# Roots on GpSimd, squares and scalings on ScalarE, and a new deal of the input rows in a two-layer hybrid encoder

## The chip, the cores and the metric

The kernel runs on one core of a Trainium2 chip. The metric is the device time of one execution in microseconds. Before the change three runs took 916.98, 917.23 and 917.36 us; the median is 917.23.

Five engines work side by side in the core: TensorE (PE in the profile; its weight loads are PEld), VectorE (DVE), ScalarE (ACT), GpSimd (POOL) and SyncE (SP), which here only issues DMAs. Each has its own queue and works it off in order. An instruction that needs another engine's result waits at the head of its queue, and all behind it wait too.

## The reference

Two layers run over x (256 tokens of 2048 features, fp32). In each layer:

```python
h = rmsnorm(x, norm_g[l])
a_x, a_b, a_c, a_g, d_q, d_k, d_v, d_g, m_q, m_g = split(h @ w_in[l])   # 4 x 768, 4 x 768, 2 x 512 columns
# A: gated convolution over three tokens
y_a = a_b * conv3(a_c * a_x) * silu(a_g)
# D: six heads; q and k are normed in halves of 64 columns
s_c = q_c @ k_c.T / 8 - slope[h] * abs(i - j)                           # c = 0, 1
o = (softmax(s_0) - lam * softmax(s_1)) @ v
y_d = rmsnorm(o, head_g) * (1 - lam_init) * silu(d_g)
# M: four heads over 256 memory tokens; mq and mk are normed over 128 columns
y_m = softmax(mq @ mk.T / sqrt(128)) @ mv * silu(m_g)
x = x + concat(y_a, y_d, y_m) @ w_out[l]
```

The memory's keys and values are rmsnorm(mem) @ w_mem_kv[l]. Every rmsnorm is v * rsqrt(mean(v * v) + 1e-6) * gain.

## The kernel before

**Products in three parts.** All large products have 128x128 stationary tiles of the turned tokens (xT, yT, memT) and 512 moving columns of weights. Each fp32 operand is split in two: hi is the value rounded to fp32r (ScalarE, L294, or L899 and L892 in the memory's phase), and lo is the rest (VectorE, raw − hi, L295, L900 and L892). Three matmuls (hi hi, hi lo, lo hi) make one product.

**Blocks and chunks.** A block is 512 output columns of 256 tokens: two PSUM accumulators `acc`, one for each row tile t, and 16 k tiles of 128 features. Weights come in chunks of two k tiles (CK = 2), 512 KB each, by a DMA on SP (L291) into one of four `raw` buffers; hi and lo have four buffers each. So SP waits until a `raw` is free, ScalarE until a hi is free, VectorE for hi, TensorE for both. Four accumulators allow two blocks to be open. Where w_in has pieces of 256 columns, a chunk is two DMAs. In some places two k tiles of two blocks are done with seven products in place of eight (`seven`); there VectorE also forms sums of the weights (L380).

**Order in time.** The memory's products come first (about 0 to 98 us), then layer 0 (to about 500 us) and layer 1. In a layer the blocks go q and k (three blocks, b = 0, 1, 2, each normed in halves of 64), v and gates, then memory queries and gates, then the convolution's groups, then w_out. Beside the blocks run side tasks, Python generators that are called forward between chunks (`later`, `run_side`); they hold the heads, the turning of x, the memory's keys. What is marked `pin` or `keep_in_program_order` stays in the order of the code on its engine; the rest is placed by a scheduler when the program is built.

**What the change touches.**
- `rsqrt` (L189 to L204): a first guess by integer steps and three Newton steps on VectorE, 11 instructions; `Steps` lets some of them run between chunks.
- `row_stats` (L414 to L422): from the sum of squares of each token, r and five multiples of it.
- `normed_steps` (L436 to L447): for q, k and the memory's queries and keys: one square of 128x512 on ScalarE for each t, a grouped sum on VectorE, the roots, and one multiplication on VectorE from PSUM to an SBUF sheet. The accumulators come free behind it.
- `diff_weights` and `diff_out` (L613 to L646): for each head, the scores with the distance term, maximum, exponentials, and their combination; then the head's own norm, times the gate.
- `mem_scores` (L651 to L680): the same for the memory's heads.
- `x_turned`, `turn_strips` (L767 to L784): x in strips of 32 rows, turned by VectorE (L770), then each of four k tiles multiplied by its gain and split (L264, L265).
- `keys` (L845 to L857): the memory's keys go out and back over GpSimd's DMA queue (L852, L853) and are then turned by VectorE (L855) into mkT.
- `row_tiles`, `x_row_tiles`, `load_w`: which row of w_in goes to which partition, and the DMA of a chunk.

Of the kernel before, what the change touches and what calls it, by code (L numbers as in the profile page):

```python
# [48 lines left out]
def encoder(ctx: ExitStack, tc: tile.TileContext, x, mem, norm_g, w_in, conv_w, conv_b,  # L49
# [128 lines left out]
    class Steps:  # L178


        def __init__(self):
            self.ops = []

        def __getattr__(self, op):
            return lambda *a, **k: self.ops.append((op, a, k))

        def run(self, n):
            for at, (op, a, k) in enumerate(self.ops):
                tc.keep_in_program_order(getattr(nc.vector, op)(*a, **k))  # L189
                if at % n == n - 1:  # L190
                    yield 1

    def rsqrt(t, n, vec=None):

        vec = vec or nc.vector
        y = small.tile([P, n], F32, tag=f"rs_y{n}", name=nm("rsy"))
        a = small.tile([P, n], F32, tag=f"rs_a{n}", name=nm("rsa"))
        yi = y.bitcast(I32)
        vec.tensor_scalar(yi, t.bitcast(I32), 1, None, ALU.logical_shift_right)
        vec.tensor_scalar(yi, yi, -1.0, float(0x5F3759DF), ALU.mult, ALU.add)  # L200
        for _ in range(3):
            vec.scalar_tensor_tensor(a, y, -0.5, y, ALU.mult, ALU.mult)
            vec.tensor_tensor(a, a, t, ALU.mult)
            vec.scalar_tensor_tensor(y, a, 1.5, y, ALU.add, ALU.mult)  # L204
        return y

# [79 lines left out]
    def load_w(rows, cols):  # L286
# [3 lines left out]
        for lo, n in cols:  # L290
            nc.sync.dma_start(raw[:, :, at:at + n], rows[:, :, lo:lo + n])  # L291
            at += n
# [137 lines left out]
    def normed_steps(vec, acc, gs, st, home):  # L430

        ng = NB // gs
        ss = small.tile([P, NT, ng], F32, tag=f"ss{ng}", name=nm("ss"))
        for t in range(NT):
            sq = tmp.tile([P, NB], F32, tag="nat", name=nm("sq"), bufs=3)
            nc.scalar.activation(sq, acc[t], AF.Square)  # L436
# [931 lines left out]
```

## Time and profile before

| | |
|---|---|
| median of three runs | 917.23 us |
| the profiled execution: its span, first to last instruction | 916.3 us |
| granted clock of TensorE | 1.000 |
| TensorE busy | 910.9 us (99%) |
| VectorE busy | 733.0 us (80%) |
| ScalarE busy | 499.0 us (54%) |
| GpSimd busy | 38.2 us (4%) |
| DMA | 215.18 MB, mean 235 GB/s |

The time of the profiled execution is known by its span alone. In rows of the profile a name such as `hi<-raw` is output and input by the program's names; `[1.67 <-PE acc L305]` is the idle time of the engine just ahead of the instruction, and what ended it. In the table of windows an engine's busy time in a stretch stands with its number of instructions in brackets. A row of waits gives microseconds in total, times, and the longest.

### The profile page before, as it was taken

How to read it: one execution, taken by the hardware profiler on the slowest of the kernel's cores; microseconds unless marked ns; L12 is line 12 of the kernel's file. 1: busy time of each engine (PE TensorE's matmuls, PEld its weight loads, DVE VectorE, ACT ScalarE, POOL GpSimd, SP SyncE). 2: the span in 40 equal slices, each digit the busy share in tenths (PEclk: the TensorE clock that was granted, in tenths of full speed). 3: DMA queues.
4: the chain of work that ended last, by engine and by line, in shares of the span. 5: the costliest groups of instructions: out<-in, count | busy, mean ns of one | idle time of the engine just before them, and what ended most of it. 6: DMA issues, size and time to landing. Idle time of an engine off the chain costs nothing.

```text
span 916.3 us, 12514 instructions
## 1 busy us (share of the span) xinstructions
PE 910.9 (99%) x4203; PEld 753.2 (82%) x4203; DVE 733.0 (80%) x1321; ACT 499.0 (54%) x778; POOL 38.2 (4%) x68
## 2 busy tenths in 40 slices
PE   9999999999999999999999999999999999999998
PEld 6888888888888888888888888888888888888887
DVE  5579978878789778677689859888888789498786
ACT  5667644546546556545556544556545556456352
POOL 2435010000000000000000000000000000000000
PEclk9999999999999999999999999999999999999999
DMA  8899888786787998979777874996869998989842
GB/s 288 289 243 256 280 247 230 227 258 185 204 228 185 271 263 242 243 253 254 240 220 232 271 243 117 280 279 197 221 192 208 258 266 256 240 243 253 280 157 93
DMA packets 244050, 215.18 MB, mean 235 GB/s; under 512 B 131976, under 2 KB 171720, under 8 KB 243984
## 3 DMA queue, kind: packets, MB, share of 16 engines
q1 hardware_dynamic: 239008, 208.71, 78.9%
q0 software_dynamic: 3776, 4.59, 2.1%
q10 hardware_dynamic: 1200, 1.07, 0.3%
q8 instruction: 33, 0.54, 0.3%
q14 instruction: 33, 0.27, 0.1%
HBM read 193.30 MB, written 21.00 MB: 234 GB/s over the span
## 4 chain that ended last, share of the span: by engine, by line
PE 98%; DMA 1%; SPq 0%; DVE 0%; ACT 0%; issue 0%
PE acc L305 90%; PE x L351 2%; PE acc L351 2%; PE po L518 1%; PE s L608 1%; DMA raw<-in_w_mem_kv_dram 1%; PE po L733 1%; PE pt L747 0%; PE s L666 0%; PE s L667 0%; PE s L665 0%; SPq L880 0%; SPq L817 0%; DVE lo L900 0%; ACT hi L899 0%; PE rest L305 0%
## 5 line engine op out<-in xcount | busy, mean ns | idle before, releaser
L305 PE MATMUL acc<-hi,xT 128*128 128x512 f32 x1760 | 550.5, 390 | 0.0
L294 ACT CAST hi<-raw 128x1024 fp32r<-128x1024 f32 x266 | 278.5, 1052 | 281.3 <-PE acc L305 187.3
L295 DVE TENSOR_TENSOR lo<-raw,hi 128x1024 fp32r<-128x1024 f32 x266 | 323.6, 1220 | 113.3 <-ACT hi L294 111.7
L305 PEld LDWEIGHTS acc<-hi,xT 128*128 128x128 f32 x1760 | 330.2, 188 | 68.8
L305 PE MATMUL acc<-lo,xT 128*128 128x512 f32 x880 | 343.0, 390 | 0.0
L305 PEld LDWEIGHTS acc<-lo,xT 128*128 128x128 f32 x880 | 165.2, 188 | 33.1
L305 PE MATMUL acc<-hi,yT 128*128 128x512 f32 (+1 forms) x432 | 134.1, 388 | 0.0
L305 PEld LDWEIGHTS acc<-hi,yT 128*128 128x128 f32 x432 | 81.0, 188 | 16.7
L305 PE MATMUL acc<-lo,yT 128*128 128x512 f32 x216 | 83.7, 388 | 0.0
L305 PE MATMUL acc<-hi,memT 128*128 128x512 f32 x248 | 78.1, 393 | 0.0
L305 PEld LDWEIGHTS acc<-hi,memT 128*128 128x128 f32 x248 | 46.1, 188 | 9.4
L900 DVE SCALAR_TENSOR_TENSOR lo<-raw,cva,hi 128x1024 fp32r<-128x1024 f32 (+1 forms) x34 | 41.0, 1220 | 14.2 <-ACT hi L899 13.8
L305 PE MATMUL acc<-lo,memT 128*128 128x512 f32 x124 | 48.0, 391 | 0.2 <-DVE lo L900 0.2
L305 PEld LDWEIGHTS acc<-lo,yT 128*128 128x128 f32 x216 | 40.5, 188 | 8.4
L899 ACT ACTIVATE hi<-raw,cva 128x1024 fp32r<-128x1024 f32 (+1 forms) x34 | 36.5, 1099 | 11.3 <-DMA raw<-in_w_mem_kv_dram 9.7
L377 ACT CAST hi<-wide 128x1024 fp32r<-128x1024 f32 x21 | 21.8, 1050 | 27.1 <-DVE wide L380 12.3
L377 DVE TENSOR_TENSOR lo<-wide,hi 128x1024 fp32r<-128x1024 f32 x21 | 25.5, 1221 | 4.3 <-ACT hi L377 4.0
L305 PEld LDWEIGHTS acc<-lo,memT 128*128 128x128 f32 x124 | 23.3, 188 | 6.0 <-DVE lo L900 1.1
L622 ACT ACTIVATE e<-e,mx 128x256 f32<-128x256 f32 x48 | 23.8, 498 | 6.2 <-DVE mx L618 6.2
L764 POOL DMA_DIRECT2D xt<-in_x_dram x32 | 21.4, 677 | 19.5 <-DVE rsy L189 13.7
L480 DVE STREAM_TRANSPOSE sh<-sh 128x1024 f32<-128x1024 f32 (+2 forms) x14 | 17.4, 1239 | 0.0
L264 ACT ACTIVATE xT<-xf,gx 128x256 fp32r<-128x256 f32 x32 | 14.3, 500 | 4.8 <-DVE xf L770 4.1
(218 smaller groups left out, 760.0 us busy)
## 6 DMA issues: line engine op xcount, KB each, us to landing
raw<-in_w_in_dram SPq DMA_DIRECT2D x188, 512.0 KB, 4.8
raw<-in_w_out_dram SPq DMA_DIRECT2D x54, 512.0 KB, 4.8
raw<-in_w_in_dram SPq DMA_DIRECT2D x64, 256.0 KB, 4.3
raw<-in_w_mem_kv_dram SPq DMA_DIRECT2D x30, 512.0 KB, 6.0
d<-sh SPq DMA_DIRECT2D x88, 128.0 KB, 4.2
sh<-d SPq DMA_DIRECT2D x72, 128.0 KB, 4.2
wide<-in_w_out_dram SPq DMA_DIRECT2D x10, 512.0 KB, 6.3
xs<-in_x_dram SPq DMA_DIRECT2D x4, 512.0 KB, 6.2
```

The lines of the kernel that those rows point to most:

```text
L264: both = (nc.scalar.activation(hi, src, AF.Copy, scale=gain), nc.vector.scalar_tensor_tensor(lo, src, gain, hi.bitcast(F32), ALU.mult, ALU ...
L294: nc.scalar.copy(hi, raw)
L295: nc.vector.tensor_tensor(lo_, raw, hi.bitcast(F32), ALU.subtract)
L305: i = nc.tensor.matmul(acc, left, right, start=start, stop=stop)
L351: nc.tensor.matmul(acc, left[a], right[b], start=first and i == 0, stop=last and i == 2)
L377: return ((hi, pin(nc.scalar.copy(hi, src))), (lo, pin(nc.vector.tensor_tensor(lo, src, hi.bitcast(F32), ALU.subtract))))
L480: tc.keep_in_program_order(nc.vector.transpose(src, src))
L518: nc.tensor.matmul(po[:, t, :], eT[:, i, t, k, :], v[:, k, h * P:(h + 1) * P], start=k == 0, stop=k == NT - 1)
L622: nc.scalar.activation(e[:, c, i], e[:, c, i], AF.Exp, bias=mx[:, c, i:i + 1], accum_out=sm[:, c, i:i + 1])
L764: tc.keep_in_program_order(nc.gpsimd.dma_start(st[:, n], src[n * B:(n + 1) * B].rearrange("p (b r) -> b p r", b=NA)))
L899: both = (nc.scalar.activation(hi[:, j], raw[:, j], AF.Copy, scale=g), nc.vector.scalar_tensor_tensor(lo[:, j], raw[:, j], g, hi[:, j].bit ...
L900: nc.vector.scalar_tensor_tensor(lo[:, j], raw[:, j], g, hi[:, j].bitcast(F32), ALU.mult, ALU.subtract))
```

## The change

It does six things.

1. **Roots.** `rsqrt` becomes one GpSimd instruction, t to the power −0.5, with a tile of −0.5 as exponent. `row_stats` moves to GpSimd with it (six instructions).
2. **Norms of q, k, mq, mk.** In place of one square of 128x512 ScalarE makes one for each group (eight of 64 columns, or four of 128), each with its sum. GpSimd makes the mean and the root for each t. ScalarE then copies each group from PSUM to the sheet with the root as scale. VectorE has nothing left in it.
3. **Heads.** ScalarE makes the distance term of a head (128x512); VectorE adds it to the scores and takes the maximum in one instruction (four of 128x256). ScalarE scales the second softmax and VectorE adds the two at once. The head's norm goes over GpSimd (add, power, multiply), its scaling to ScalarE, and one VectorE multiplication with the gate is left. In the memory's heads the factor 1/sqrt(128) goes into a gain, and ScalarE scales the weights.
4. **Rows of w_in.** Within each group of 512 rows, partition 32 b + p of k tile j holds row 128 b + 32 j + p where it held row 4 (32 b + p) + j. The strips of x are then turned from contiguous columns, and norm_g is loaded by four DMAs and turned by VectorE.
5. **Strips of x.** Four gains in place on ScalarE, then one copy and one subtraction of 128x1024 for the whole strip, where each k tile had its own.
6. **Loads.** Each k tile of a chunk has its own DMA: 242 loads of 512 KB become two of 256 KB each, and 64 of 256 KB become two of 128 KB each.

In the built program TensorE has 4,155 matmuls before and after. ScalarE goes from 605 rows of the listing to 776, GpSimd from 36 to 155, and VectorE from 1,247 to 864 (a row can stand for several equal instructions).

**Where the order changes.** The first place is ScalarE at the first q block of layer 0. `hi` are the casts of weights, `sq` the squares, `acc` the block's accumulators, `sh` the sheet. Before:

```order
L294 CAST hi_1245<-raw_1243 128x1024
L294 CAST hi_1263<-raw_1261 128x1024
L294 CAST hi_1281<-raw_1279 128x1024
L436 ACTIVATE sq_1215<-acc_1061 128x512
L436 ACTIVATE sq_1219<-acc_1062 128x512
L294 CAST hi_1299<-raw_1297 128x1024
L294 CAST hi_1323<-raw_1321 128x1024
L294 CAST hi_1341<-raw_1339 128x1024
```

After the change:

```order
L276 CAST hi_1347<-raw_1344 128x1024
L418 ACTIVATE sq_1229,ss_1205<-acc_1050 128x64
L418 ACTIVATE sq_1231,ss_1205<-acc_1050 128x64
L418 ACTIVATE sq_1233,ss_1205<-acc_1050 128x64
L426 ACTIVATE sh_1243<-acc_1049,rs_1206 128x2x32 x3
L418 ACTIVATE sq_1235,ss_1205<-acc_1050 128x64
L426 ACTIVATE sh_1243<-acc_1049,rs_1206 128x2x32 x5
L276 CAST hi_1366<-raw_1363 128x1024
L418 ACTIVATE sq_1237,ss_1205<-acc_1050 128x64
L418 ACTIVATE sq_1239,ss_1205<-acc_1050 128x64
L276 CAST hi_1385<-raw_1382 128x1024
L426 ACTIVATE sh_1243<-acc_1050,rs_1206 128x2x32 x8
```

The scaled copies, which wait for GpSimd's root `rs`, now stand between the casts: those of the first tile behind squares of the second, those of the second tile behind a cast.

The second place is GpSimd's queue at the end of the memory's phase. `xt` are strips of x, `kd` and `sh` the way of the memory's keys out and back. Before:

```order
L764 DMA xt_716<-in_x_dram 128x1x128 x8
L764 DMA xt_801<-in_x_dram 128x1x128 x8
L852 DMA kd_928<-sh_617 32x4x256 x4
L853 DMA sh_617<-kd_928 128x1024
L852 DMA kd_1315<-sh_1028 32x4x256 x4
L853 DMA sh_1028<-kd_1315 128x1024
```

After the change:

```order
L419 TENSOR_SCALAR ss_1020<-ss_1020,stm_491 128x4
L188 TENSOR_TENSOR rs_1021<-ss_1020,root 128x4
L419 TENSOR_SCALAR ss_1205<-ss_1205,st_1040 128x8
L188 TENSOR_TENSOR rs_1206<-ss_1205,root 128x8
L419 TENSOR_SCALAR ss_1205<-ss_1205,st_1040 128x8
L188 TENSOR_TENSOR rs_1206<-ss_1205,root 128x8
L826 DMA kd_1300<-sh_1086 32x4x256 x4
L827 DMA sh_1086<-kd_1300 128x1024
L419 TENSOR_SCALAR ss_1421<-ss_1421,st_1040 128x8
L188 TENSOR_TENSOR rs_1422<-ss_1421,root 128x8
L419 TENSOR_SCALAR ss_1421<-ss_1421,st_1040 128x8
L188 TENSOR_TENSOR rs_1422<-ss_1421,root 128x8
```

The second layer's keys (`kd_1300`) now stand behind the roots of the first q block (`rs_1206`), where they stood directly behind the first layer's.

The third place is VectorE where the memory's phase ends. `lo` are the conversions for the first block of layer 0 (lo_979 and lo_1002 before, lo_976 and lo_1001 after are its chunks 0 and 1), `mkT` is the turn of the first layer's keys. Before:

```order
L422 TENSOR_TENSOR st_1038<-rsy_1041 128x2
L892 TENSOR_TENSOR lo_1002<-raw_976,hi_1001 128x1024
L770 STREAM_TRANSPOSE xf_1019<-xt_801 128x1024
L189 TENSOR_REDUCE ss_1021<-sq_1022 128x4
L892 TENSOR_TENSOR lo_1098<-raw_982,hi_1097 128x1024
L189 TENSOR_SCALAR ss_1021<-ss_1021,stm 128x4
L189 TENSOR_REDUCE ss_1021<-sq_1024 128x4
L892 TENSOR_TENSOR lo_1117<-raw_984,hi_1116 128x1024
L855 STREAM_TRANSPOSE mkT_111<-sh_617 128x1024
```

After the change:

```order
L875 SCALAR_TENSOR_TENSOR lo_957<-raw_929,cva,hi_956 128x1024
L762 TENSOR_TENSOR xT_112<-xf_911,xT_112 128x1024
L867 TENSOR_TENSOR lo_976<-raw_953,hi_975 128x1024
L829 STREAM_TRANSPOSE mkT_113<-sh_670 128x1024
L867 TENSOR_TENSOR lo_1001<-raw_972,hi_1000 128x1024
L748 STREAM_TRANSPOSE xf_1018<-xt_802 128x1024
L867 TENSOR_TENSOR lo_1092<-raw_979,hi_1091 128x1024
```

The turn of the keys moved from behind chunk 3 to between chunks 0 and 1.

The last place is SP in layer 1, where the 256-column blocks begin. `raw` are chunks of weights, the rest are sheets on their way through DRAM. After the change:

```order
L473 DMA d_6912<-sh_6501 32x4x256 x4
L477 DMA mqT_6243<-d_6912 128x8x32 x4
L273 DMA raw_7050<-in_w_in_dram 128x1x256 x4
L477 DMA yn_6554<-d_6995 128x4x32 x4
L273 DMA raw_7077<-in_w_in_dram 128x1x256 x4
L273 DMA raw_7104<-in_w_in_dram 128x1x256 x4
L273 DMA raw_7144<-in_w_in_dram 128x1x256 x4
L273 DMA raw_7165<-in_w_in_dram 128x1x256 x4
L473 DMA d_7186<-sh_7000 32x4x256 x4
L273 DMA raw_7191<-in_w_in_dram 128x1x256 x4
```

Each `raw` there is now four DMAs of 128 KB, where it was two of 256 KB.

The diff, cut to its core:

```diff
...
+BIG = 3.0e38
...
     def load_norm():
-        tc.keep_in_program_order(nc.gpsimd.dma_start(gx.rearrange("p (m j) -> p m j", j=QT),
-                                                     norm_g.rearrange("l (q p j) -> p (l q) j", p=P, j=QT)))
+        rows = norm_g.rearrange("l (q b j p) -> b (l q) j p", b=NA, j=QT, p=B)
+        for b in range(NA):
+            pin(nc.gpsimd.dma_start(gx[b * B:(b + 1) * B], rows[b]))
+        yield 4
+        pin(nc.vector.transpose(gx, gx))
...
-    def rsqrt(t, n, vec=None):
...
+    root = const.tile([P, NT * NB // HALF], F32, name="root")
+    nc.gpsimd.memset(root, -0.5)
+    def rsqrt(r, t):
+        n = t.shape[-1]
+        nc.gpsimd.tensor_tensor(r, t, root[:, 0:n], ALU.pow)
...
     def row_tiles(w, k):
-        return w[k * P:(k + CK) * P].rearrange("(j p) c -> p j c", p=P)
+        return [w[(k + j) * P:(k + j + 1) * P] for j in range(CK)]
     def x_row_tiles(w, k, n=CK):
         q, j = divmod(k, QT)
-        return w[q * NB:(q + 1) * NB].rearrange("(p j) c -> p j c", j=QT)[:, j:j + n]
+        tiles = w[q * NB:(q + 1) * NB].rearrange("(b j p) c -> b p j c", j=QT, p=B)
+        return [tiles[:, :, j + i] for i in range(n)]
...
         raw = raw_tile()
         at = 0
         for lo, n in cols:
-            nc.sync.dma_start(raw[:, :, at:at + n], rows[:, :, lo:lo + n])
+            for j, row in enumerate(rows):
+                nc.sync.dma_start(raw[:, j, at:at + n], row[..., lo:lo + n])
             at += n
...
+    R, HR, HR2, R2, ET = range(5)
     def row_stats(ss, tag):
-        st = keep.tile([P, 6, NT], F32, tag=tag, name=nm(tag))
+        st = keep.tile([P, 5, NT], F32, tag=tag, name=nm(tag))
         t = small.tile([P, NT], F32, tag="st_t", name=nm("stt"))
...
+        nc.gpsimd.tensor_scalar(t, ss, 1.0 / D_MODEL, EPS, ALU.mult, ALU.add)
+        rsqrt(st[:, R], t)
+        nc.gpsimd.tensor_scalar(st[:, ET], t, EPS, None, ALU.mult)
+        nc.gpsimd.tensor_scalar(st[:, HR], st[:, R], 0.5, None, ALU.mult)
+        nc.gpsimd.tensor_tensor(st[:, R2], st[:, R], st[:, R], ALU.mult)
+        nc.gpsimd.tensor_scalar(st[:, HR2], st[:, R2], 0.5, None, ALU.mult)
         return st
     def col(st, which, t):
         return st[:, which, t:t + 1]
-    def normed_steps(vec, acc, gs, st, home):
-        ng = NB // gs
+    def normed_steps(acc, gs, st, home):
+        ng, w = NB // gs, gs // B
         ss = small.tile([P, NT, ng], F32, tag=f"ss{ng}", name=nm("ss"))
+        r = small.tile([P, NT, ng], F32, tag=f"rs{ng}", name=nm("rs"))
         for t in range(NT):
-            sq = tmp.tile([P, NB], F32, tag="nat", name=nm("sq"), bufs=3)
-            nc.scalar.activation(sq, acc[t], AF.Square)
-            vec.tensor_reduce(ss[:, t], sq.rearrange("p (g d) -> p g d", d=gs), AX.X, ALU.add)
-            vec.tensor_scalar(ss[:, t], ss[:, t], col(st, R2_64 if gs == HALF else R2_128, t), EPS,
-                              ALU.mult, ALU.add)
-        r = rsqrt(ss.rearrange("p t g -> p (t g)"), NT * ng, vec).rearrange("p (t g) -> p t g", t=NT)
+            for g in range(ng):
+                sq = small.tile([P, gs], F32, tag="sq", name=nm("sq"), bufs=1)
+                nc.scalar.activation(sq, acc[t][:, g * gs:(g + 1) * gs], AF.Square, accum_out=ss[:, t, g:g + 1])
+            nc.gpsimd.tensor_scalar(ss[:, t], ss[:, t], 1.0 / gs, col(st, ET, t), ALU.mult, ALU.add)
+            rsqrt(r[:, t], ss[:, t])
+            yield 1
         both = home()
         for t in range(NT):
...
+            for g in range(ng):
+                j, b = divmod(g * w, NA)
+                nc.scalar.activation(both[:, b:b + w, j, t], strips(acc[t][:, g * gs:(g + 1) * gs]), AF.Copy,
+                                     scale=r[:, t, g:g + 1])
+            yield 1
         return both
...
     def diff_weights(l, h, s):
+        al = tmp.tile([P, NT, SEQ], F32, tag="nat", name=nm("al"), bufs=3)
+        nc.scalar.activation(al, dist, AF.Copy, scale=-slopes[h])
         e = tmp.tile([P, 2, NT, SEQ], F32, tag="e", name=nm("e"))
+        mx = small.tile([P, 2, NT], F32, tag="mx", name=nm("mx"))
         for c in range(2):
-            nc.vector.scalar_tensor_tensor(e[:, c], dist, -slopes[h], s[c], ALU.mult, ALU.add)
-        mx = small.tile([P, 2, NT], F32, tag="mx", name=nm("mx"))
-        nc.vector.tensor_reduce(mx, e, AX.X, ALU.max, negate=True)
+            for i in range(NT):
+                nc.vector.tensor_tensor_reduce(e[:, c, i], s[c][:, i], al[:, i], -1.0, BIG, ALU.add, ALU.min,
+                                               mx[:, c, i:i + 1])
         sm = small.tile([P, 2, NT], F32, tag="sm", name=nm("sm"))
         for c in range(2):
             for i in range(NT):
-                nc.scalar.activation(e[:, c, i], e[:, c, i], AF.Exp, bias=mx[:, c, i:i + 1],
+                nc.scalar.activation(e[:, c, i], e[:, c, i], AF.Exp, bias=mx[:, c, i:i + 1], scale=-1.0,
                                      accum_out=sm[:, c, i:i + 1])
-        iv = small.tile([P, 2, NT], F32, tag="iv", name=nm("iv"), bufs=6)
-        nc.vector.reciprocal(iv, sm)
         cf = small.tile([P, NT], F32, tag="cf", name=nm("cf"))
-        nc.vector.scalar_tensor_tensor(cf, sm[:, 0], neglam[:, l:l + 1], iv[:, 1], ALU.mult, ALU.mult)
+        nc.vector.reciprocal(cf, sm[:, 1])
+        nc.vector.scalar_tensor_tensor(cf, sm[:, 0], neglam[:, l:l + 1], cf, ALU.mult, ALU.mult)
         for i in range(NT):
-            nc.vector.scalar_tensor_tensor(e[:, 0, i], e[:, 1, i], cf[:, i:i + 1], e[:, 0, i], ALU.mult, ALU.add)
-        return e[:, 0], iv
-    def diff_out(h, yn, po, iv, st, a):
+            nc.scalar.activation(e[:, 1, i], e[:, 1, i], AF.Copy, scale=cf[:, i:i + 1])
+        nc.vector.tensor_tensor(e[:, 0], e[:, 1], e[:, 0], ALU.add)
+        floor = small.tile([P, NT], F32, tag="iv", name=nm("floor"), bufs=6)
+        nc.gpsimd.tensor_tensor(floor, sm[:, 0], sm[:, 0], ALU.mult)
+        nc.gpsimd.tensor_scalar(floor, floor, EPS, None, ALU.mult)
+        return e[:, 0], floor
+    def diff_out(h, yn, po, floor, st, a):
         ss = small.tile([P, NT], F32, tag="hss", name=nm("hss"))
+        z = tmp.tile([P, NT, P], F32, tag="z", name=nm("hz"))
         for i in range(NT):
-            sq = tmp.tile([P, P], F32, tag="z", name=nm("hsq"))
-            nc.scalar.activation(sq, po[:, i, :], AF.Square, accum_out=ss[:, i:i + 1])
...
+        nc.gpsimd.tensor_tensor(ss, ss, floor, ALU.add)
+        rsqrt(r, ss)
+        nc.gpsimd.tensor_tensor(r, r, st[:, HR], ALU.mult)
         for i in range(NT):
-            nc.vector.scalar_tensor_tensor(yn[:, :, i], strips(po[:, i, :]), r[:, i:i + 1],
-                                           strips(a[:, i, h * P:(h + 1) * P]), ALU.mult, ALU.mult)
+            nc.scalar.activation(z[:, i], po[:, i, :], AF.Copy, scale=r[:, i:i + 1])
+        nc.vector.tensor_tensor(yn.rearrange("p b t c -> p t b c"), z.rearrange("p t (b c) -> p t b c", c=B),
+                                a[:, :, h * P:(h + 1) * P].rearrange("p t (b c) -> p t b c", c=B), ALU.mult)
...
     def turn_strips(st):
         whole = tmp.tile([P, QT, SEQ], F32, tag="sh", name=nm("xf"))
         tc.keep_in_program_order(nc.vector.transpose(whole.rearrange("p j (n i) -> p j n i", i=B),
-                                                     st.rearrange("p n (c j) -> p j n c", j=QT)))
+                                                     st.rearrange("p n (j c) -> p j n c", c=B)))
         return whole
     def x_turned(dst, l, q, src, after=None, wait=2):
...
         whole = turn_strips(st)
         yield
         for j in range(QT):
-            split_T(dst, q * QT + j, whole[:, j], g_norm(l, q * QT + j), pin=True)
-            if j % 2:
-                yield
+            pin(nc.scalar.activation(whole[:, j], whole[:, j], AF.Copy, scale=g_norm(l, q * QT + j)))
+        hi, lo = (dst[:, part, q * QT:(q + 1) * QT] for part in range(2))
+        pin(nc.scalar.copy(hi, whole))
+        pin(nc.vector.tensor_tensor(lo, whole, hi.bitcast(F32), ALU.subtract))
+        made.update((id(dst), q * QT + j) for j in range(QT))
+        yield
...
     def mem_stats():
...
+        stm.append(stats_of(ssm, "stm"))
+        yield
...
```

In the memory's heads `mgain` takes P ** -0.5, one VectorE scaling of the maximum goes, and the weights are scaled by `nc.scalar.activation(e[:, i], e[:, i], AF.Copy, scale=r[:, i:i + 1])`.

More of the change, by code (lines that the diff above doesn't have):

```diff
@@ L176, in __getattr__ @@
             return lambda *a, **k: tc.keep_in_program_order(getattr(nc.vector, op)(*a, **k))
[L178 to L191, printed above, removed]
-    def rsqrt(t, n, vec=None):
[L195 to L205, printed above, removed]
+    root = const.tile([P, NT * NB // HALF], F32, name="root")
[3 more added lines that the diff above has]
+        nc.gpsimd.tensor_tensor(r, t, root[:, 0:n], ALU.pow)
     side, tasks = deque(), []
@@ L449, in normed_steps @@
-        return both
-    def normed(acc, gs, st, home):
-        return normed_steps(nc.vector, acc, gs, st, home)
-    def normed_slowly(acc, gs, st, home):
-        vec = Steps()
-        both = normed_steps(vec, acc, gs, st, home)
-        yield from vec.run(3)
-        return both
+            for g in range(ng):
+                j, b = divmod(g * w, NA)
+                nc.scalar.activation(both[:, b:b + w, j, t], strips(acc[t][:, g * gs:(g + 1) * gs]), AF.Copy,
+                                     scale=r[:, t, g:g + 1])
@@ L463, in sheet, with normed @@
+            yield 1
+        return both
+    def normed(*how):
+        steps = normed_steps(*how)
+        try:
+            while True:
+                next(steps)
+        except StopIteration as end:
+            return end.value
     def sheet(home, tag, n=NB // P):
@@ L637, in diff_out @@
-        t = small.tile([P, NT], F32, tag="ht", name=nm("ht"))
-        nc.vector.scalar_tensor_tensor(t, ss, 1.0 / P, iv[:, 0], ALU.mult, ALU.mult)
-        nc.vector.tensor_tensor(t, t, iv[:, 0], ALU.mult)
-        nc.vector.tensor_scalar(t, t, EPS, None, ALU.add)
-        r = rsqrt(t, NT)
-        nc.vector.tensor_tensor(r, r, iv[:, 0], ALU.mult)
-        nc.vector.tensor_tensor(r, r, st[:, HR], ALU.mult)
+            nc.scalar.activation(z[:, i], po[:, i, :], AF.Square, scale=P ** -0.5, accum_out=ss[:, i:i + 1])
@@ L660, in mem_scores @@
         yield 1
-        sc = P ** -0.5
         s = ps_s.tile([P, NT, SEQ], F32, tag="s", name=nm("s"))
@@ L678, in mem_scores @@
         for i in range(NT):
-            nc.vector.tensor_scalar(e[:, i], e[:, i], r[:, i:i + 1], None, ALU.mult)
+            nc.scalar.activation(e[:, i], e[:, i], AF.Copy, scale=r[:, i:i + 1])
         return e
@@ L828, in mem_stats @@
     def mem_stats():
-        vec = Steps()
-        t = small.tile([P, NT], F32, tag="ssum", name=nm("ssum"))
-        y = stm[0]
-        vec.tensor_reduce(t, ssm, AX.X, ALU.add)
-        vec.tensor_scalar(t, t, 1.0 / D_MODEL, EPS, ALU.mult, ALU.add)
-        r = rsqrt(t, NT, vec=vec)
-        vec.tensor_copy(y[:, R], r)
-        vec.scalar_tensor_tensor(y[:, R2_128], r, 1.0 / P, r, ALU.mult, ALU.mult)
-        yield from vec.run(6)
+        stm.append(stats_of(ssm, "stm"))
+        yield
     def mem_keys(l, kraw):
-        nat = yield from normed_slowly([kraw[:, t] for t in range(NT)], P, stm[0], sheets("v"))
+        nat = yield from normed_steps([kraw[:, t] for t in range(NT)], P, stm[0], sheets("v"))
         yield 6
@@ L874, in load @@
             if l == DEPTH:
-                pin(nc.sync.dma_start(self.raw[s], x_row_tiles(w_in[0], k * CK)[:, :, C_D:C_D + NB]))
+                for j, row in enumerate(x_row_tiles(w_in[0], k * CK)):
+                    pin(nc.sync.dma_start(self.raw[s][:, j], row[..., C_D:C_D + NB]))
                 return
@@ L981, in beside @@
             if k == 9:
-                load_norm()
+                tasks.append(later(load_norm(), 0))
             if k == 11:
```

26 lines of the change are left out of this document (5 added, 21 removed).

## The prediction

> **What bounds the kernel now.** I read the page's busy times first, then TensorE's waits, then the chain of work that ended last, and only then the stages.
>
> ```profile
> span 916.3 us, 12514 instructions
> PE 910.9 (99%) x4203; PEld 753.2 (82%) x4203; DVE 733.0 (80%) x1321; ACT 499.0 (54%) x778; POOL 38.2 (4%) x68
> PE 98%; DMA 1%; SPq 0%; DVE 0%; ACT 0%; issue 0%
> ```
>
> TensorE is busy for 910.9 of 916.3 us, and the chain lies on it for 98%. All its waits that the view of waits shows for it are these (microseconds in total, times, longest):
>
> ```profile
> PE warm L128 <- DVE zeros L123: 1.2, 1, 1.2
> PE acc L917 <- ACT hi L899: 0.4, 1, 0.4
> PE acc L305 <- DVE lo L900: 0.2, 1, 0.2
> ```
>
> That is 1.8 us. The other 3.6 us of the 5.4 that TensorE is not busy are the launch before its first instruction and the last adds and the store behind its last one. So the other engines do not set the time; they only have to be early enough. How early, a row of the chain and two groups tell:
>
> ```profile
> 46.94 130.61 PE acc L305 x576
> L294 ACT CAST hi<-raw 128x1024 fp32r<-128x1024 f32 x266 | 278.5, 1052 | 281.3 <-PE acc L305 187.3
> L295 DVE TENSOR_TENSOR lo<-raw,hi 128x1024 fp32r<-128x1024 f32 x266 | 323.6, 1220 | 113.3 <-ACT hi L294 111.7
> ```
>
> 130.61 / 576 is 0.227 us for a matmul, and a chunk of weights (two k tiles, each with two row tiles and three products) is 12 of them: 2.72 us. For each chunk ACT casts for 1.05 us and DVE subtracts for 1.22 us. Four pairs of hi and lo exist, and ACT's idle time ahead of the casts ends mostly with TensorE (187.3 of 281.3 us), when it frees a pair: the cast for the chunk four further on starts then, three chunks (8.2 us) before it is needed. Less 1.05 and 1.22, a finished conversion leads by 5.9 us. That is the cushion that any delay must first use up. It is thinner where ACT or DVE has little left in a stage:
>
> ```profile
> core 0: us, PE busy (x) PEld busy (x) DVE busy (x) ACT busy (x) POOL busy (x), PEclk, DMA share, GB/s
> 62.00:98.00 36.00, 36.00 (x160) 29.80 (x159) 32.44 (x70) 26.72 (x46) 13.54 (x21) 1.00 0.88 259
> 120.00:164.00 44.00, 44.00 (x195) 36.41 (x195) 35.43 (x65) 20.91 (x24) 0.99 (x2) 1.00 0.83 242
> 164.00:190.00 26.00, 26.00 (x116) 21.50 (x115) 24.84 (x42) 13.87 (x16) 0.00 (x0) 1.00 0.76 215
> 552.00:580.00 28.00, 28.00 (x124) 23.02 (x123) 25.28 (x44) 13.53 (x15) 0.00 (x0) 1.00 0.55 157
> 900.00:917.00 17.00, 12.69 (x65) 10.69 (x63) 9.53 (x18) 1.58 (x2) 0.00 (x0) 0.99 0.20 65
> ```
>
> In the stages at 62, 164 and 552 us DVE has 90 to 96% of the time filled. TensorE is busy throughout all the same, at a granted clock of 1.00.
>
> **The change, part by part.** TensorE keeps the same 4,155 matmuls of the built program; a few change places. Therefore nothing in its 910.9 us goes, and a gain could only come out of 5.4 us, most of it the launch and the end:
>
> ```profile
> 912.73 0.42 DVE L1274 TENSOR_TENSOR xs<-rest,xs 128x256 f32<-128x256 f32 x1 [0.32 <-PE rest L305]
> ```
>
> This last add and its store are left as they are. The work taken from DVE is worth nothing for the same reason: it lies beside TensorE. What remains is to ask of each added thing whether the cushion covers it.
>
> *ACT's small squares and scalings.* Rows for them:
>
> ```profile
> L436 ACT ACTIVATE sq<-acc 128x512 f32<-128x512 f32 x12 | 7.2, 600 | 5.8 <-PE acc L305 5.3
> L636 ACT ACTIVATE hsq<-po 128x128 f32<-128x128 f32 x24 | 6.3, 267 | 0.0
> L636 ACT ACTIVATION_READ_ACCUMULATOR hsq<-po 128x1 f32 x24 | 4.7, 197 | 0.0
> L1222 ACT ACTIVATE sh<-acc,st 128x512 f32<-128x512 f32 x8 | 5.3, 685 | 1.6 <-PE acc L305 1.6
> L1222 ACT ACTIVATE sh<-acc,st 128x256 f32<-128x256 f32 x8 | 3.8, 476 | 2.9 <-PE acc L305 2.8
> L264 ACT ACTIVATE xT<-xf,gx 128x256 fp32r<-128x256 f32 x32 | 14.3, 500 | 4.8 <-DVE xf L770 4.1 <-DVE rsy L189 0.7
> ```
>
> Squares go by (600 − 267) / 384 = 0.87 ns per column: 64 columns take 0.21 us, with a separate accumulator read 0.41; I take 0.30. Scalings go by (685 − 476) / 256 = 0.82 ns: 64 columns take 0.32, 128 columns 0.37. A q or k block then costs ACT 16 × 0.30 + 16 × 0.32 − 2 × 0.60 = 8.7 us more. Two such blocks fall in 120 to 164 us: 20.9 + 17.4 = 38.3 of 44. One each in the stages at 164 and 552 us: 22.6 of 26 and 22.2 of 28. It fits everywhere, and DVE becomes looser in the same stages. The tightest is 62 to 98 us, with one block of keys and three strips of x: eight scalings (3.0), four more squares with read (4 × 0.46 = 1.8), less one square of 0.6, and three copies of a strip (3 × 1.05 = 3.2) come to 34.1 of 36. That stage is where the waits of 0.4 and 0.2 us are: it has no cushion to speak of, but DVE loses about as much there as ACT gains. I allow 0.2 us, with 0 and 2 us (about what ACT has left) as ends.
>
> *Roots on GpSimd.* They replace chains of 11 small DVE steps; a step is this:
>
> ```profile
> L202 DVE SCALAR_TENSOR_TENSOR rsa<-rsy 128x2 f32<-128x2 f32 x42 | 6.6, 158 | 0.3
> L104 POOL COPY vb<-memT 128x1 f32<-128x1 f32 x1 | 0.2, 184 | 16.1 <-ACT memT L261 16.1
> L79 POOL IOTA dist<- 128x512 f32 x1 | 0.6, 562 | 0.0
> ```
>
> No row shows a power on GpSimd. From below it costs as much as the small copy, 0.18 us; from above I set eight passes of the longest compute row, 8 × 0.56 = 4.5. In size (8 columns at most) it is nearest to the small rows, as an operation to none; so 1.0, towards the lower end. Its two-step chain (scale, power) is 1.2 us, within 0.4 and 4.7; the three-step chain of a head (add, power, multiply) 1.4, within 0.5 and 4.9. ACT waits for them in line with its casts: if scalings stand at once behind the squares, the next cast is late by the chain. In a q block the squares of the second tile and a cast stand between (the order shown above), about 2.5 us. In four of the twelve heads nothing stands between, and ACT stalls for 1.4 us; the 5.9 us of cushion cover that, and a third of it would. At the upper end 4.9 us are covered only by a full cushion. I take 0.
>
> *Queue of GpSimd and the keys of the memory.* The second layer's key DMAs now stand behind the roots of the first q block, and DVE's turn of the first layer's keys moves ahead of the conversion of chunk 1:
>
> ```profile
> 118.26 2.18 POOL L852 DMA_DIRECT2D kd<-sh  x4 [24.49 <-DVE sh L189]
> 93.20 0.57 POOL L853 DMA_DIRECT2D sh<-kd  x1 [5.33 <-DMA kd<-sh]
> 125.05 0.56 POOL L853 DMA_DIRECT2D sh<-kd  x1 [4.61 <-DMA kd<-sh]
> DMA to landing us min/median/max: 4.0/5.2/7.4
> 97.81 1.23 DVE L892 TENSOR_TENSOR lo<-raw,hi 128x1024 fp32r<-128x1024 f32 x1 [0.61 <-ACT hi L892]
> 104.46 1.24 DVE L855 STREAM_TRANSPOSE mkT<-sh 128x1024 f32<-128x1024 f32 x1
> 101.68 0.39 PE L305 MATMUL acc<-lo,xT 128*128 128x512 f32 x1
> ```
>
> Here chunk 1's lo (of the first block of layer 0, which starts near 98.5) was finished at 99.04, 2.6 us before its first use at 101.68. Now it waits for the keys' landing: 93.20 + 5.2 = 98.4, at worst 100.6, then a turn of 1.24 and the subtraction of 1.22: 100.9, at worst 103.1. So nothing at the median, 1.4 us at worst, and more if the statistics on GpSimd hold back the DMA at 93.20. I take 0.3. The second group of DMAs starts some 11 us later (four chunks, over which the q block's squares and roots are spread); the keys are back at 125.05 + 11 + 5.2 = 141.3. Their turn stands on DVE behind the conversion of chunk 1 of the third block; that block starts two blocks of 8 × 2.72 us behind 98.5, at 142.0, so this conversion ends near 142.0 + 2.7 − 5.9 = 138.8. DVE stands still for up to 2.5 us, under a full cushion: 0.
>
> *Loads.* The 242 loads of 512 KB become pairs of 256 KB, and 64 of 256 KB become pairs of 128 KB: 306 more issues on SP.
>
> ```profile
> SPq L291 <- DVE lo L295: 219.8, 106, 10.0
> 706.33 5.29 SPq L291 DMA_DIRECT2D raw<-in_w_in_dram  x8
> raw<-in_w_in_dram SPq DMA_DIRECT2D x188, 512.0 KB, 4.8
> raw<-in_w_in_dram SPq DMA_DIRECT2D x64, 256.0 KB, 4.3
> ```
>
> At 5.29 / 8 = 0.66 us that is up to 202 us of issuing, against 219.8 us in which SP waits for a free buffer. On the whole it is hidden; a chunk's second half leaves 0.66 us later, under 5.9: 0. [...] By the two rows above, half the bytes land in 4.3 instead of 4.8 us.
>
> *The rest* (scores and maximum in one DVE step, strips turned from contiguous rows, the norm gains in four DMAs) takes work off DVE or moves it to ACT beside TensorE: 0; without cover the scalings of the weights would cost 0.5 us for each of 40. In all ACT gains 6 × 8.7 (q and k) + 4 × (8 × 0.46 + 8 × 0.37 − 1.2) (memory keys and queries) + 8 × 1.05 (strips) + 12 × (0.69 + 2 × 0.50 + 2 × 0.37) (heads) + 16 × 0.50 (memory weights) = 119 us and comes to 618; DVE loses 25 roots of 11 × 0.16 = 44 us by these alone, and comes below 690.
>
> **Sum:** 0.2 + 0.3 = 0.5 us on the span: 916.3 + 0.5 = 916.8. The median lies 0.9 above the span (917.23 − 916.3); so 917.7.
>
> **Rivals.** *A, the roots come late (slower).* If the power costs 2 us or more, a head's stalled ACT makes casts late, and where the cushion is the 2.6 us of chunk 1 instead of 5.9, TensorE starves. At the upper price, with two of the four bare heads at such thin places: 2 × (4.9 − 2.6) = 4.6, so 917.2 + 4.6 = 921.8. It decides from a three-step chain of 2.6 us on. For it: an unknown operation whose result ACT awaits in order. Against: most places have work between. [...]
>
> *B, loads late at the 256-column blocks.* There a chunk is four issues, 1.3 us more on SP, and four such chunks follow the carries in a row.
>
> ```profile
> 712.67 1.05 ACT L294 CAST hi<-raw 128x1024 fp32r<-128x1024 f32 x1 [2.65 <-DMA raw<-in_w_in_dram]
> ```
>
> ACT already waited 2.65 us for a load there, which leaves 5.9 − 2.65 = 3.3. Three chunks late make 3.9, so 0.6 lost at each of four blocks: 2.4, 919.6. Against: the buffers are filled ahead of the carries.
>
> *C, faster.* Needs matmuls that run quicker, for the waits give 1.8 us at most; all 5.4 us gone would be 911.8, half of it 914.5. The clock is 1.00 already.
>
> **How the numbers follow.** Forecast, no change: 0.64, itself 916.4 to 919.0. A 0.21, B 0.10, C 0.05. A measurement tells about 0.2% (1.8 us), so A and B count as slower (0.31), C as faster. The time is 917.7. The range starts at 916.4 (the small waits at TensorE gone, 0.8) and ends at 922.5, above A; outside stay C and an A with a power far above 4.5 us.
>
> **What would show it.** Right: TensorE's busy time within 1 us of 910.9, its waits in all under 3 us, DVE below 690 and ACT near 618 us busy, GpSimd's small steps at 1 us or less. Wrong on the roots: ACT's scalings waiting for GpSimd by over 2.6 us, and behind them TensorE waiting for lo. Wrong on the loads: casts waiting longer for loads at the 256-column blocks, and TensorE after them. Wrong on the keys: a wait of TensorE near 101 us. A shorter matmul than 0.227 us would show C.

## The result, and the profile after

The changed kernel takes 1595.26 us (median of four runs, 1592.65 to 1596.91) against 917.3 before: a ratio of 1.738, with a 95% interval of 1.736 to 1.741. The prediction was 917.7. It is wrong by 678 us, and none of its three rivals named the cause.

The page of the changed kernel, in the rows that answer to those shown of before:

```profile
span 1593.4 us, 13237 instructions
PE 1187.1 (75%) x4203; PEld 857.1 (54%) x4203; DVE 637.0 (40%) x878; ACT 592.7 (37%) x1226; POOL 113.7 (7%) x190
SPq 42%; DMA 32%; PE 15%; ACT 4%; DVE 4%; issue 2%; POOL 0%; ACTq 0%; DVEq 0%
```

The chain that ended last no longer lies on TensorE (98% before) but on SP's queue and the DMAs (74%). Its engines' waits, in microseconds in total, times and longest:

```profile
ACT hi L276 <- DMA raw<-in_w_in_dram: 688.1, 173, 8.7
ACT hi L276 <- DMA raw<-in_w_out_dram: 14.2, 7, 5.3
PE acc L287 <- ACT hi L276: 232.0, 130, 6.0
```

ScalarE's casts wait 688 us for loads of w_in, and TensorE waits for the casts. For loads of w_out, which are halved in the same way, the casts wait 14 us. Before, the first of these rows was:

```profile
ACT hi L294 <- DMA raw<-in_w_in_dram: 60.3, 35, 6.3
```

The windows say the same by stage:

```profile
core 0: us, PE busy (x) PEld busy (x) DVE busy (x) ACT busy (x) POOL busy (x), PEclk, DMA share, GB/s
62.00:98.00 36.00, 36.00 (x160) 29.55 (x159) 24.34 (x31) 29.57 (x58) 19.83 (x30) 1.00 0.75 228
200.00:500.00 300.00, 211.18 (x733) 147.23 (x732) 105.24 (x158) 109.27 (x269) 19.08 (x33) 0.84 0.33 111
880.00:1480.00 600.00, 418.02 (x1378) 289.22 (x1378) 196.69 (x278) 198.72 (x455) 29.76 (x46) 0.83 0.36 113
```

The kernel before in a stretch of layer 0:

```profile
200.00:500.00 300.00, 300.00 (x1417) 249.42 (x1416) 242.66 (x439) 166.03 (x280) 0.00 (x0) 1.00 0.83 234
```

In the memory's phase TensorE is full as before. Where w_in is read, the sixteen DMA engines are busy for a third and move 111 to 113 GB/s, half of before. So the sixteen engines as a whole are not full, and yet the loads are late. The view of the DMAs over 12 us, in forty slices, shows how. First a stretch of before (150 to 162 us), then one of the changed kernel (330 to 342 us) in which nothing but loads of w_in runs:

```profile
DMA  9999999999614857997300000094599960495638
GB/s 375 403 376 375 416 430 369 396 416 403 266 62 96 123 116 225 355 430 307 130 14 0 0 0 0 0 116 75 171 314 410 403 253 7 41 102 48 68 130 314
```

```profile
DMA  2222222222222222222222222222222222222222
GB/s 109 89 109 102 102 96 109 102 102 96 109 102 102 96 109 102 102 96 109 102 102 96 102 109 96 102 102 109 96 102 102 109 89 109 102 109 89 109 102 102
q1 hardware_dynamic: 618, 1.23, 26.3%
```

Before, the loads came in bursts near 400 GB/s with pauses between, as buffers came free (SP waits for them 219.8 us in all). Now there is no pause and no burst: a constant 102 GB/s at 26.3% of sixteen engines, which is the time of four engines (4.2). The packets of the trace confirm it: one of 2 KB takes 84 ns, as the median before. Of 600 instants of this stretch, 0.02 us apart, exactly four packets are under way at 476, and five or six at the others. The casts arrive at that pace:

```profile
330.24 1.04 ACT L276 CAST hi<-raw 128x1024 fp32r<-128x1024 f32 x1 [4.10 <-DMA raw<-in_w_in_dram]
335.35 1.05 ACT L276 CAST hi<-raw 128x1024 fp32r<-128x1024 f32 x1 [4.07 <-DMA raw<-in_w_in_dram]
340.50 1.04 ACT L276 CAST hi<-raw 128x1024 fp32r<-128x1024 f32 x1 [4.10 <-DMA raw<-in_w_in_dram]
```

A chunk comes every 5.1 us, and TensorE needs 2.72. What is different about these loads is the pattern by which they read w_in. This is the source of one k tile's load, as pairs of step (in elements) and count, from the outside in; the destination is 128 partitions of 512 columns in both:

```
rows dealt as before:   [28672, 128] [1, 512]
rows dealt anew:        [917504, 4] [7168, 32] [1, 512]
```

With the old deal, partition p holds row 4p + j: one step for all 128 partitions. With the new one partition 32b + p holds row 128b + 32j + p: 4 runs of 32 rows. The theory F of the experiments is that a load whose outermost dimension is 4 is spread over 4 DMA engines, 32 packets each, 32 × 0.08 = 2.6 us for 256 KB. I had not thought of it before the result. The rivals: I, that the doubled number of issues on SP does it; D, that the new order of rows is slow to read in DRAM, whatever the engines; R, that the roots and scalings come late.

### The profile page after: what moved, and what is told of

Same layout as the page of the kernel before. It is cut to its first block, busy times and chain, and to the rows that moved or that the text cites. A ratio compares the mean times of both kernels' runs of the same rounds, so it can differ in the third digit from the quotient of the medians.

```text
span 1593.4 us, 13237 instructions
## 1 busy us (share of the span) xinstructions
PE 1187.1 (75%) x4203; PEld 857.1 (54%) x4203; DVE 637.0 (40%) x878; ACT 592.7 (37%) x1226; POOL 113.7 (7%) x190
## 4 chain that ended last, share of the span: by engine, by line
SPq 42%; DMA 32%; PE 15%; ACT 4%; DVE 4%; issue 2%; POOL 0%; ACTq 0%; DVEq 0%
SPq L273 26%; DMA raw<-in_w_in_dram 23%; PE acc L287 12%; SPq L477 12%; DMA d<-sh 5%; SPq L473 3%; DVE lo L277 2%; ACT hi L276 2%; DMA wide<-in_w_in_dram 1%; DMA d<-yn 1%; PE x L333 1%; SPq L850 1%; DMA xd<-xs 1%; PE acc L333 1%; ACT hi L874 0%
## 5 line engine op out<-in xcount | busy, mean ns | idle before, releaser
L287 PE MATMUL acc<-hi,xT 128*128 128x512 f32 x1760 | 707.2, 473 | 238.9 <-ACT hi L276 232.0
L287 PEld LDWEIGHTS acc<-hi,xT 128*128 128x128 f32 x1760 | 402.6, 230 | 388.8 <-ACT hi L276 295.0
L287 PE MATMUL acc<-lo,xT 128*128 128x512 f32 x880 | 430.4, 489 | 115.3 <-DVE lo L277 110.8
L287 PEld LDWEIGHTS acc<-lo,xT 128*128 128x128 f32 x880 | 201.7, 229 | 228.4 <-DVE lo L277 180.9
L419 POOL TENSOR_SCALAR ss<-ss,st 128x8 f32<-128x8 f32 (+1 forms) x16 | 10.7, 669 | 336.7 <-ACT sq L418 336.7
L188 POOL TENSOR_TENSOR rs<-ss,root 128x8 f32<-128x8 f32 (+1 forms) x20 | 28.2, 1412 | 1.7
L494 PE MATMUL po<-v,sh 128*128 128x128 f32 x96 | 15.3, 305 | 16.6 <-DVE mx L596 9.1
```

What stands on the lines that cost most here:

```text
L188: nc.gpsimd.tensor_tensor(r, t, root[:, 0:n], ALU.pow)
L287: i = nc.tensor.matmul(acc, left, right, start=start, stop=stop)
```

## The experiments

**Undo the deal alone, keep all else.** The halved loads, the roots, norms, heads and strips stay as in the change.

```diff
-        tiles = w[q * NB:(q + 1) * NB].rearrange("(b j p) c -> b p j c", j=QT, p=B)
-        return [tiles[:, :, j + i] for i in range(n)]
+        tiles = w[q * NB:(q + 1) * NB].rearrange("(p j) c -> p j c", j=QT)
+        return [tiles[:, j + i] for i in range(n)]
```

(and the strips and norm_g to match)

> The whole change, but with the rows of w_in dealt as before (partition p of k tile j takes row 4 p + j of its group of 512), x turned from strided columns and norm_g loaded as before. Every k tile still has a DMA of its own, so SP issues as many loads as in the change. Theory F (four engines): with the new deal the source of a w_in load has an outermost dimension of 4 (four runs of 32 rows), and its 128 packets go over 4 of the 16 DMA engines, 32 each; a 256 KB load then takes 32 x 0.08 = 2.6 us and a chunk 5.1 us, where TensorE needs 2.72. Here the outermost dimension is 128 again, so the loads are quick: 917 to 919 us. Theory I (twice as many issues on SP): as slow as the change, about 1595. Theory R (roots and scalings come late): as slow as the change, about 1595. Theory D (the new order of rows in DRAM is slow to read, however many engines read it): 917 to 919.

Measured: 919.31 us, ratio 1.0015 to before (1.0006 to 1.0024). The time falls by 676 us with the old deal back, and SP issues as many loads as in the change. I and R fall. TensorE is back on the path. The page's busy times, and then all waits of TensorE:

```profile
PE 910.3 (99%) x4203; PEld 752.7 (82%) x4203; DVE 638.3 (70%) x877; ACT 587.9 (64%) x1226; POOL 123.6 (13%) x187
```

```profile
PE warm L130 <- DVE zeros L125: 1.2, 1, 1.2
PE acc L285 <- DVE lo L873: 0.8, 2, 0.6
PE acc L890 <- ACT hi L872: 0.2, 1, 0.2
```

**Do the deal alone.** The kernel before, with the new deal and a DMA for each k tile of w_in. Loads of w_out stay whole.

```diff
-            nc.sync.dma_start(raw[:, :, at:at + n], rows[:, :, lo:lo + n])
+            for j, row in enumerate(rows):   # w_in: [4][32] rows for each k tile; w_out as before
+                nc.sync.dma_start(raw[:, j, at:at + n], row[..., lo:lo + n])
...
```

(and x_row_tiles, the strips and norm_g as in the change)

> The kernel before with one part of the change alone: the new deal of w_in's rows, with a DMA for each k tile of w_in, the strips turned from contiguous columns and norm_g loaded to suit. Roots, norms, heads and w_out's loads are as before. Theories F and D: the loads bind, 1560 to 1600 us, with 4 DMA engines busy in the stages of w_in. Theory I: some 242 more issues in place of 306, so well above 917 too, 1300 to 1500. Theory R: 917 to 919.

Measured: 1631.71 us. It is enough by itself. It is also 36 us slower than the whole change, and 32 above the range I gave: once the loads bind, the rest of the change helps. VectorE's work, which is 733.5 us here and 637.0 there, ends each buffer's use; that this is the reason was not tried.

**Keep the deal, change the shape of the load.** Every row goes to the same place from the same address, but by four DMAs of 32 partitions for each chunk.

```diff
-            for j, row in enumerate(rows):
-                nc.sync.dma_start(raw[:, j, at:at + n], row[..., lo:lo + n])
+            for b, part in zip((0, 2, 1, 3), rows):          # part: 32 rows x 2 k tiles
+                nc.sync.dma_start(raw[b * B:(b + 1) * B, :, at:at + n], part[..., lo:lo + n])
```

(and x_row_tiles, the loads of the first block and those into `wide` to match)

> The change with the new deal kept, every byte to the same place, but each chunk of w_in loaded by four DMAs, one for each group of 32 partitions (both k tiles at once, 128 KB), so that the outermost dimension is 32. Theory F: all 16 engines work again; SP issues four times for 512 columns (about 1.8 us of 2.72) and eight times where a chunk has two pieces of 256 (about 3.6 us, for 32 chunks at most 0.9 us short each): 918 to 945 us. Theory I: still more issues, slower than 1595. Theory D: the same rows in the same order, about 1595. Theory R: about 1595.

Measured: 987.89 us, ratio 1.076 (1.075 to 1.078). The same scattered rows are read 607 us faster, so D falls. The range (918 to 945) was missed by 43 us. The trace shows one new bound, SP itself, in the blocks where a chunk has two pieces of 256 columns and so eight DMAs. A row of SP's timeline, and TensorE's two largest waits:

```profile
415.05 10.19 SPq L274 DMA_DIRECT2D raw<-in_w_in_dram  x21
```

```profile
PE acc L291 <- ACT hi L280: 18.3, 15, 3.0
PE acc L291 <- DVE lo L281: 16.7, 37, 0.8
```

10.19 us for 21 issues is 0.49 each, so eight of them take 3.9 us against TensorE's 2.72, where I had reckoned 3.6. But TensorE waits 40.6 us in all, and only about 23 of them lie in the four stretches in which such chunks are issued, up to 12 us behind them; it is also busy for 30 us longer, 940.9 us, at a mean granted clock of 0.987. I had left out that the carries are issued on the same queue; how much of the rest is theirs was not separated. So I's mechanism exists, with this price, only not in the change.

**Leave the loads out.** Rows and loads as before, all the rest of the change.

```diff
-            for j, row in enumerate(rows):
-                nc.sync.dma_start(raw[:, j, at:at + n], row[..., lo:lo + n])
+            nc.sync.dma_start(raw[:, :, at:at + n], rows[:, :, lo:lo + n])
```

(and row_tiles, x_row_tiles, the strips and norm_g as before)

> The whole change without anything on the loads: rows dealt as before, one DMA for a chunk as before, x turned from strided columns, norm_g as before. Roots on GpSimd, squares and scalings on ScalarE, heads and strips as in the change. By the prediction's sum, without its terms for the loads: 917.7 us, within 0.2% of before. Theory R: 1595, or at least above 921.

Measured: 918.84 us, ratio 1.0012 (1.0003 to 1.0020), 0.85 us above the 917.99 of before beside it. The sum of the prediction, 0.5 us, is within this run's interval, but not by the terms that it was added up from: in the profiled execution TensorE waits 4.9 us where it waited 1.8, and is busy for 1.4 us less (909.5). That the sum comes out so near is partly luck. TensorE's waits, ScalarE's longest for GpSimd, and the groups of GpSimd:

```profile
PE acc L283 <- DVE lo L273: 1.3, 1, 1.3
PE warm L130 <- DVE zeros L125: 1.2, 1, 1.2
PE acc L887 <- ACT hi L869: 0.8, 1, 0.8
PE acc L329 <- ACT hi L355: 0.8, 1, 0.8
PE acc L283 <- DVE lo L870: 0.8, 2, 0.5
```

```profile
ACT hz L620 <- POOL ht L618: 12.9, 9, 2.1
```

```profile
L186 POOL TENSOR_TENSOR rs<-ss,root 128x8 f32<-128x8 f32 x12 | 20.4, 1702 | 1.0
L186 POOL TENSOR_TENSOR ht<-hss,root 128x2 f32<-128x2 f32 x12 | 10.2, 851 | 0.9
L415 POOL TENSOR_SCALAR ss<-ss,st 128x8 f32<-128x8 f32 x12 | 8.4, 704 | 117.8 <-ACT sq L414 117.8
L616 POOL TENSOR_TENSOR hss<-hss,floor 128x2 f32<-128x2 f32 x12 | 6.4, 530 | 93.1 <-ACT hz L614 93.1
L618 POOL TENSOR_TENSOR ht<-ht,st 128x2 f32<-128x2 f32 x12 | 4.3, 354 | 0.9
```

**Other numbers of runs.** If the outermost dimension sets the engines, the time must follow it. Three kernels take a k tile in 2, 8 or 16 runs instead of 4.

```diff
-        tiles = w[q * NB:(q + 1) * NB].rearrange("(b j p) c -> b p j c", j=QT, p=B)
+        tiles = w[q * NB:(q + 1) * NB].rearrange("(b j p) c -> b p j c", j=QT, p=P // G)   # G = 2, 8, 16
```

> The change with one thing altered: a k tile of w_in is taken from its group of 512 rows in 2 runs of 64 rows where the change has 4 runs of 32. Sizes, packets and the number of issues stay; the rows no longer meet the right features of x, so the result is not the reference's, and the run is for its time alone. Theory F: 2 of 16 engines, 64 packets x 0.08 = 5.1 us for 256 KB, a DMA share near 0.125 and 52 GB/s in the stages of w_in; in the change w_in takes about 188 x 5.1 + 32 x 5.9 + 4 x 5.1 = 1168 us on four engines, here twice that, so 1595 + 1168 = 2760, between 2600 and 2900 us. Theory D (the reading of scattered rows in DRAM): fewer and longer runs, so faster than 1595. Theory I: 1595.

> As the run with 2, but 8 runs of 16 rows (for its time alone). Theory F: 8 engines, 1.3 us for 256 KB and 2.6 us for a chunk, just under TensorE's 2.72, and 2.9 where a chunk has pieces of 256 columns: 918 to 990 us. Theory D: shorter runs, slower than 1595. Theory I: 1595.

> As the run with 2, but 16 runs of 8 rows (for its time alone). Theory F: all 16 engines, 917 to 920 us. Theory D: still shorter runs, slower than with 8. Theory I: 1595.

| outermost dimension | time (us) | runs |
|---|---|---|
| 2 | 2740.65 | 1 |
| 4 (the change) | 1595.26 | 4 |
| 8 | 1044.74 | 1 |
| 16 | 932.99 | 2 |
| 128 (old deal, halved loads) | 919.31 | 11 |

D's order is the other way round: more and shorter runs are faster. For 2 the expectation (2760) is met within 1%. From 2 and 4 alone, a time of A/k + B has A = 4 × (2740.65 − 1595.26) = 4582 and B = 450; for 8 that gives 1023, and 1045 was measured. The range for 8 (918 to 990) was too low: I set the loads' 2.6 us a chunk against TensorE's 2.72 and left out again the carries on the same queue, whose way back at L477 is 7% of that run's chain; that they make up the whole miss was not tried. In a stretch of the run with 2 (400 to 412 us), and one of the run with 8 (273 to 285 us):

```profile
DMA packets 193, 0.63 MB, mean 53 GB/s; under 512 B 8, under 2 KB 49, under 8 KB 193
q1 hardware_dynamic: 193, 0.63, 12.9%
```

```profile
q1 hardware_dynamic: 1239, 2.38, 51.9%
```

12.9% of sixteen is two engines, 51.9% a little over eight. The run with 16 stays 14 us above 128, past the 920 expected; TensorE waits 10.4 us there (2.2 with 128) and is busy for 5.3 us longer. Why 16 is not quite as good as 128 is open.

**The second k tile on another queue.** If each load in flight had its own four engines, two would fill eight; in the change the trace shows four (26.3% of sixteen). Is it the queue that ties them together?

```diff
-                nc.sync.dma_start(raw[:, j, at:at + n], row[..., lo:lo + n])
+                (nc.sync if j == 0 or len(row.shape) < 3 else nc.scalar).dma_start(raw[:, j, at:at + n], row[..., lo:lo + n])
```

(`len(row.shape) < 3` keeps w_out's loads on SP; for the second run nc.gpsimd in place of nc.scalar)

> The change with its new deal and its four-run loads, but the second k tile of each chunk of w_in is loaded by a DMA on ScalarE's queue instead of SP's. Same bytes, places and shapes. It asks why two loads in flight do not run on different engines. Theory F1 (a load of four runs always takes the same 4 DMA engines, whichever queue issues it): no gain, 1560 to 1660 us. Theory F2 (each queue, or each load, takes its own 4): the two tiles run side by side, 2.6 us for a chunk, and the time falls to 950 to 1200 us.

> [...] F1 in its strict form (any queue takes the same 4 engines): 1560 to 1700 us. F2, or a different choice of engines by GpSimd's queue: half the bytes stay on 4 engines (584 us of load for both layers by the 1168 us worked out for the change), the others go elsewhere: 950 to 1250 us, of which some by roots and loads waiting for one another on GpSimd.

Measured: 1571.04 us with ScalarE's queue (one run), 1287.86 with GpSimd's (one run). In 330 to 342 us of the first, by queue:

```profile
q1 hardware_dynamic: 314, 0.62, 13.4%
q10 hardware_dynamic: 302, 0.60, 12.9%
```

Together 26.3%, no more than SP's queue had alone in the change: a second queue brings the loads no more engines, as F1 expects. In 300 to 312 us of the second, in which nothing but loads of w_in is issued:

```profile
q0 software_dynamic: 861, 0.83, 25.1%
q1 hardware_dynamic: 450, 0.89, 20.4%
```

Together 45.5% of sixteen, the time of 7.3 engines and so more than four: with GpSimd's queue (q0) others are busy too. The run lies between the two ranges. In this stretch GpSimd's queue moves 0.83 of 1.72 MB, but its DMAs stand in one queue with the roots; how much each costs was not separated.

## Why the prediction was wrong, point by point

**The step that failed is the paragraph on loads.** It priced the split of each load by its number of issues on SP (right: hidden, as the run with the old deal shows) and by the landing time of halves (4.3 against 4.8 us). Both rows are of loads whose rows lie at one step. The new deal changes that as well, and I counted it only as "turned from contiguous rows". What the runs showed in its place: with 4 runs of 32 rows the loads fill 26.3% of sixteen DMA engines, the time of four, a chunk comes every 5.1 us instead of 2.72, and the term set to 0 was 676 us (1595.26 with the new deal, 919.31 without).

How it adds up: at 5.1 us a chunk instead of 2.72, 188 chunks of 512 columns lose about 450 us. The 32 chunks of two 256-column pieces take, as an estimate, 4 × 32 × 0.046 = 5.9 us by their 1 KB packets (46 ns each at the median of the changed kernel's trace) and lose about 100. The remaining 130 or so are not split up. The chain points to the carries, which now stand behind loads on SP: the way back at L477 is 12% of it, and an issue of a load takes longer. In the view of the tile `raw` of the changed kernel (300 to 400 us; duration as minimum, median and maximum in ns):

```profile
L273 SPq DMA_DIRECT2D raw<-in_w_in_dram x37: 531/2378/4398, 299.0 to 396.8; - x37
```

A median issue takes 2.38 us; with the old deal it is 0.43 in the same 100 us.

**The pattern was there to be weighed.** The outermost count of the source, 128 with the old deal and 4 with the new, could be read from the diff, and I did not compare the two. The runs show what it is worth: 12.9%, 26.3% and 51.9% of sixteen engines, and 2740.65, 1595.26 and 1044.74 us, for 2, 4 and 8. Halving alone, the run with the old deal against the one with old loads, is 919.31 against 918.84 us, and their runs overlap. That the loads from SP and ScalarE use the very same four engines fits the run with two queues (26.3% together), but engine numbers are not in the trace.

**What bounds the kernel** was right: with quick loads TensorE is busy 910.3 us and waits 2.2.

**Roots on GpSimd.** By their means in the run with old loads the power takes 1.70 us for eight columns, 1.42 for four and 0.85 for two, where I took 1.0 of 0.18 to 4.5, and the small steps of the heads and q blocks take 0.27 to 0.70, where I took 0.2. The means hide two prices. In the view of the tile `ht` (minimum, median and maximum in ns), and in one of its twelve heads with the VectorE subtraction beside it:

```profile
L186 POOL TENSOR_TENSOR ht<-hss,root x12: 694/695/1572, 263.2 to 744.6; 128x2 f32<-128x2 f32 x12
L618 POOL TENSOR_TENSOR ht<-ht,st x12: 196/198/1088, 263.9 to 745.4; 128x2 f32<-128x2 f32 x12
```

```profile
294.88 1.23 DVE L273 TENSOR_TENSOR lo<-raw,hi 128x1024 fp32r<-128x1024 f32 x1 [0.46 <-ACT hi L272]
295.07 1.09 POOL L618 TENSOR_TENSOR ht<-ht,st 128x2 f32<-128x2 f32 x1
```

The multiplication takes 0.20 us by itself; this one began during a subtraction and ended 0.05 us after it. In this run 37 GpSimd steps began during such a subtraction, and every one ended after it; in the changed kernel 28 did, and all of them ended after it too. VectorE shows no sign of it, for a lo takes 1.22 us on average with the change's roots and without, and 1.235 at most against 1.230.

A head's three steps take 1.8 us at the median (1.4 predicted), but 3.2 and 3.1 in two heads, past rival A's point of 2.6. ScalarE waits 12.9 us for them in all, about 1.35 in each of those two heads, and TensorE does not wait there: the cushion held. TensorE waits 0.8 us once behind the roots of a q block, at 182 us.

**ScalarE's small work** was priced a little high in sum: 590 us against 618. Squares of 64 columns with their reads follow each other every 0.35 us (0.30 taken), but scalings of 64 columns in a row every 0.20 to 0.24 (0.32 taken). In 62 to 98 us of the run with old loads ScalarE has 30.8 of 36 us, not 34.1, and TensorE waits 0.5 us there, at 77 us, where I allowed 0.2.

**The keys.** The first layer's came 1.1 us late for their turn in the run with old loads, and chunk 1's lo was ready 2.2 us ahead of its use: 0, not 0.3. The second layer's keys are where this paragraph failed. From the chain of this run and from its timeline:

```profile
129.90 1.54 POOL rs L186
131.49 0.65 POOL kd L822
139.91 6.35 DMA sh<-kd
```

```profile
146.28 1.25 DVE L825 STREAM_TRANSPOSE mkT<-sh 128x1024 f32<-128x1024 f32 x1 [6.15 <-DMA sh<-kd]
148.89 0.50 PE L283 MATMUL acc<-lo,xT 128*128 128x512 f32 x1 [1.34 <-DVE lo L273]
```

Behind the roots the keys started back 14.9 us later than before (139.91 against 125.05), where I reckoned 11, and landed at 146.3, where I reckoned 141.3. VectorE stood still for 6.15 us (I reckoned up to 2.5), longer than the full cushion of 5.9, and TensorE waited 1.34 us, its longest wait in this run, where I took 0. In the run with the old deal the same turn waited 4.4 us and TensorE did not wait.

**Rival B** had the right queue and the wrong reason: loads late because of SP's time. That happened only with four DMAs for a chunk.

## What to carry to other kernels

When an edit touches how rows are dealt to partitions, write down the pattern of the DMA's source, before and after, ahead of anything else: its outermost count was worth more than size, number or order of the transfers here (2, 4, 8 and 16 gave 2741, 1595, 1045 and 933 us; halving the loads alone, 919.31 against 918.84). Take a landing time only from a row whose pattern has the same shape: here two times of 4.3 and 4.8 us, from rows with one step for all partitions, stood behind a term of 0 that came to 676 us. And work taken off an engine beside a full TensorE was worth nothing here: with the old loads VectorE is busy for 93 us less, and the time is 0.12% longer.
